# Reordering the first loads of a strided-attention kernel: keys, first Q block, values, and 8 KiB runs for two blocks

## The chip, the cores and the metric

The kernel runs on one core of a Trainium2 chip. Its engines have short names in the profile: PE multiplies matrices, DVE and POOL work on vectors, ACT applies functions such as exp, and SP issues the DMAs, the transfers between the chip's memory and the core. 16 DMA engines share each large transfer; a transfer has *landed* when all of them have reported their share. The metric is the device time of one execution in microseconds (us). Its profile has a span a little shorter than that time (128.5 us of 130.28 us in the profiled run of the kernel before). Times are medians of several executions. A ratio is the mean time of one kernel's fast runs divided by the mean time of the other's fast runs of the same rounds, so it is not quite the ratio of the medians quoted.

## The reference

```python
batch, heads, seq, dim = (8, 12, 1024, 64)          # Q, K, V: float32, stride = 64
scale = 1.0 / np.sqrt(dim)
for i in range(seq):                                # every query
    attend_positions = np.arange(0, seq, stride)    # ... sees the same 16 positions
    scores  = einsum('bhqd,bhkd->bhqk', q_i, k[attend_positions]) * scale
    weights = softmax(scores)                       # max subtracted, 1e-10 in the denominator
    result[:, :, i, :] = einsum('bhqk,bhkd->bhqd', weights, v[attend_positions])
```

Q and the result are 25.2 MB each. Of K and V only 16 rows per head are used, 0.39 MB each, but each row is a run of only 256 bytes. Per byte moved there is little arithmetic.

## The kernel before

The 96 heads are taken in 24 groups of four. Per group the kernel loads 1 MiB of Q, transposes it on PE, forms scores, takes exp on ACT, sums and multiplies by the values on PE, scales on DVE and stores 1 MiB. All DMAs are issued by SP, in program order, on one queue. Eleven Q buffers let eleven loads be issued ahead.

```python
kv_src = [[stride * D, P], [2 * HG * SD, NC], [1, D]]       # 128 x 12 runs of 256 bytes
nc.sync.dma_start(k_raw, _ap_with(K, kv_src))
nc.sync.dma_start(v_raw, _ap_with(V, kv_src))
def load(g):                                                # 1 MiB of Q in 32 runs of 32 KiB
    qn[g] = qn_pool.tile([P, 32 * D], FP32, name="qn", tag="qn")
    _copy(nc, qn[g], _ap_with(Q, [[HG * SD // 32, 32], [1, HG * SD // 32]], g * HG * SD))
for g in range(QBUFS):                                      # QBUFS = 11
    load(g)
# ... on POOL: identity, perm_k, k_dup (needs K), perm_v, v_bf (needs V), iota (leads to mask) ...
# ... PE: kp from k_dup; then vp from v_bf, four matmuls with two PSUM buffers,
#     each emptied by four DVE instructions (v_bd) that also need mask ...
for g in range(2):
    for x in range(2):
        transposes(g, x)                                    # PE, then an ACT copy to qt
scores(0)                                                   # PE, then exp on ACT
for g in range(NG):                                         # NG = 24
    sums(g)
    outputs(g, 0)
    outputs(g, 1)
    if g + 1 < NG:
        scores(g + 1)
    # ... outputs(g, 2), outputs(g, 3), transposes(g + 2, 0 and 1) ...
    store(g)                                                # 1 MiB
    if g + QBUFS < NG:
        load(g + QBUFS)
```

The softmax here doesn't subtract the row's maximum and nothing guards it: scores larger than these inputs give would overflow.

## Time and profile before

| | before |
|---|---|
| median of all its runs beside the changed kernel's first six | 130.32 us (130.23 to 130.45) |
| span of the profiled run | 128.5 us |
| busiest compute engine | ACT, 67% of the span |
| DMA engines' packet time | 96.3% of 16 engines' span |
| first store issued | 25.18 us |
| last DVE instruction ends | 114.22 us |

These are the page's slices of the kernel before (40 equal slices of 3.2 us; a digit is the busy share in tenths, GB/s is what the 16 DMA engines moved) and its queue table (packets, MB, share of 16 engines' span).

```profile
DVE  6229963787677777787777877877877778750000
ACT  2163294988889888898888898888988888400000
DMA  2999989999899899999999999999998999999980
GB/s 57 351 398 418 449 367 490 388 423 439 339 421 487 357 441 439 413 434 449 383 467 426 393 459 428 393 469 421 405 469 357 416 434 416 421 428 421 434 337 23
q1 hardware_dynamic: 7712, 51.12, 96.3%
q8 instruction: 7, 0.11, 0.4%
q14 instruction: 3, 0.02, 0.0%
```

The DMA row is full from the second slice on, and it goes on for three slices after DVE has stopped. The last two rows are instruction fetches, and the page counts them among the packets of the 16 DMA engines.

The start of the kernel and the end of its compute, from the timelines of SP, POOL, PE and DVE (start in us, duration in us, engine, line, operation, operands; in brackets the idle time before it and what ended it):

```profile
1.99 12.62 SPq L34 DMA_DIRECT2D qn<-in_Q_dram  x11
5.06 1.60 POOL L116 CAST k_dup<-k_raw 128x768 bf16<-128x768 f32 x2 [3.04 <-DMA k_raw<-in_K_dram]
7.80 0.83 POOL L124 CAST v_bf<-v_raw 128x768 bf16<-128x768 f32 x1
9.68 8.49 DVE L180 TENSOR_SCALAR v_bd<-vp,mask 128x384 bf16<-128x384 f32 x16
14.29 1.91 PE L193 MATMUL qt_ps<-identity,qn 128*128 128x128 bf16 x16
25.18 0.63 SPq L34 DMA_DIRECT2D out_dram<-out_sb  x1
111.74 2.48 DVE L243 TENSOR_TENSOR out_sb<-o_ps,rec 128x512 f32<-128x512 f32 x4
```

The last row is the end of DVE's work (111.74 + 2.48 = 114.22 us). The cast of V starts without a wait, because POOL was still busy when V landed. The first transposes start at 14.29 us although Q block 0 had landed at 9.2 us: PE issues the fourth value matmul first, and that waits for DVE.

The chain of waits of this kernel, and the longest waits of SP (waiter, what it waited for, us in total, times, longest):

```profile
ACT 60%; PE 13%; DVE 5%; DMA 3%; POOL 3%; issue 2%; ACTq 1%; DVEq 0%; POOLq 0%
SPq L34 <- DMA qn<-in_Q_dram: 25.3, 15, 2.0
SPq L34 <- DMA out_dram<-out_sb: 22.6, 13, 2.0
SPq L34 <- DVE out_sb L243: 20.0, 12, 3.3
SPq L34 <- DVE rec L231: 19.3, 7, 8.8
SPq L307 <- DMA out_dram<-out_sb: 12.6, 1, 12.6
```

The chain names ACT, but the last line decides: after everything has been computed and issued, SP waits 12.6 us for stores to land. The chain followed compute back from the last instruction and doesn't see the backlog of DMA work. Compute has slack, and the DMA engines have none.

### The profile page before, as it was taken

How to read it: one execution, taken by the hardware profiler on the slowest of the kernel's cores; microseconds unless marked ns; L12 is line 12 of the kernel's file. 1: busy time of each engine (PE TensorE's matmuls, PEld its weight loads, DVE VectorE, ACT ScalarE, POOL GpSimd, SP SyncE). 2: the span in 40 equal slices, each digit the busy share in tenths (PEclk: the TensorE clock that was granted, in tenths of full speed). 3: DMA queues.
4: the chain of work that ended last, by engine and by line, in shares of the span. 5: the costliest groups of instructions: out<-in, count | busy, mean ns of one | idle time of the engine just before them, and what ended most of it. 6: DMA issues, size and time to landing. Idle time of an engine off the chain costs nothing.

```text
span 128.5 us, 2215 instructions
## 1 busy us (share of the span) xinstructions
PE 69.4 (54%) x880; PEld 51.1 (40%) x880; DVE 83.7 (65%) x144; ACT 86.3 (67%) x103; POOL 5.1 (4%) x23
## 2 busy tenths in 40 slices
PE   0071665975656866558766578665687655510000
PEld 0040542754445654445544456443465444300000
DVE  6229963787677777787777877877877778750000
ACT  2163294988889888898888898888988888400000
POOL 4470000000000000000000000000000000000000
PEclk9999997799999999999999999999999999955555
DMA  2999989999899899999999999999998999999980
GB/s 57 351 398 418 449 367 490 388 423 439 339 421 487 357 441 439 413 434 449 383 467 426 393 459 428 393 469 421 405 469 357 416 434 416 421 428 421 434 337 23
DMA packets 7722, 51.26 MB, mean 399 GB/s; under 512 B 3872, under 2 KB 3872, under 8 KB 3872
## 3 DMA queue, kind: packets, MB, share of 16 engines
q1 hardware_dynamic: 7712, 51.12, 96.3%
q8 instruction: 7, 0.11, 0.4%
q14 instruction: 3, 0.02, 0.0%
HBM read 25.95 MB, written 25.17 MB: 398 GB/s over the span
## 4 chain that ended last, share of the span: by engine, by line
ACT 60%; PE 13%; DVE 5%; DMA 3%; POOL 3%; issue 2%; ACTq 1%; DVEq 0%; POOLq 0%
ACT qt L198 34%; ACT w L218 26%; PE sc L206 8%; DVE v_bd L180 3%; DMA k_raw<-in_K_dram 3%; PE qt_ps L193 2%; PE o_ps L238 2%; DVE out_sb L243 1%; POOL k_dup L116 1%; POOL perm_v L120 1%; PE sm L227 1%; POOL v_bf L124 1%; ACTq L307 1%; DVEq L307 0%; PE vp L175 0%
## 5 line engine op out<-in xcount | busy, mean ns | idle before, releaser
L243 DVE TENSOR_TENSOR out_sb<-o_ps,rec 128x512 f32<-128x512 f32 x96 | 63.3, 688 | 15.3 <-PE o_ps L238 12.9
L198 ACT COPY qt<-qt_ps 128x1024 bf16<-128x1024 bf16 x48 | 46.2, 1015 | 5.2 <-PE qt_ps L193 4.7
L218 ACT ACTIVATE w<-sc 64x512 bf16<-64x512 f32 x48 | 35.4, 737 | 13.2 <-PE sc L206 12.9
L238 PE MATMUL o_ps<-v_bd,w 128*128 128x256 bf16 x192 | 33.4, 278 | 0.6 <-DVE out_sb L243 0.6
L193 PE MATMUL qt_ps<-identity,qn 128*128 128x128 bf16 x384 | 30.7, 227 | 0.2 <-ACT qt L198 0.2
L193 PEld LDWEIGHTS <-qn 128*128 128x128 bf16 x384 | 27.0, 102 | 3.9 <-issue 2.6
L206 PE MATMUL sc<-qt,k_t 128*32 128x512 bf16 x96 | 9.8, 395 | 24.5 <-ACT qt L198 24.5
L238 PEld LDWEIGHTS <-w 128*128 128x128 bf16 x192 | 14.3, 98 | 6.9 <-issue 6.2
L206 PEld LDWEIGHTS <-k_t 128*32 128x32 bf16 x96 | 4.4, 93 | 29.3 <-issue 29.2
L231 DVE RECIPROCAL rec<-sm 128x32 f32<-128x32 f32 x24 | 8.6, 358 | 9.0 <-PE sm L227 9.0
L227 PE MATMUL sm<-s_sel,w 128*128 128x4 bf16 x192 | 8.5, 166 | 6.9 <-ACT w L218 6.9
L227 PEld LDWEIGHTS <-w 128*128 128x128 bf16 x192 | 6.4, 96 | 11.0 <-ACT w L218 11.0
L180 DVE TENSOR_SCALAR v_bd<-vp,mask 128x384 bf16<-128x384 f32 x16 | 8.5, 608 | 0.1
L166 ACT CAST k_t<-kp 64x512 bf16<-64x512 f32 x6 | 3.5, 579 | 3.6 <-PE kp L160 3.5
L160 PE MATMUL kp<-perm_k,k_dup 128*128 128x128 bf16 x12 | 1.5, 312 | 6.7 <-POOL k_dup L116 6.7
L175 PE MATMUL vp<-v_bf,perm_v 128*128 128x384 bf16 x4 | 1.8, 490 | 4.6 <-DVE v_bd L180 4.1
L160 PEld LDWEIGHTS <-k_dup 128*128 128x128 bf16 x12 | 1.2, 145 | 6.7 <-POOL k_dup L116 6.7
L138 DVE TENSOR_SCALAR slot_i<-iota_p 128x1 int16<-128x1 int16 x1 | 0.2, 156 | 4.7 <-POOL iota_p L136 4.7
L166 ACT ACT_TABLE_LOAD x1 | 1.3, 1283 | 2.5 <-DVE k_t L127 2.5
L127 DVE MEMSET k_t<- 128x1536 uint32 x1 | 1.3, 1338 | 1.1 <-PEq L293 1.1
L175 PEld LDWEIGHTS <-perm_v 128*128 128x128 bf16 x4 | 0.5, 127 | 3.7 <-issue 3.7
L116 POOL CAST k_dup<-k_raw 128x768 bf16<-128x768 f32 x2 | 1.6, 827 | 3.0 <-DMA k_raw<-in_K_dram 3.0
(15 smaller groups left out, 6.0 us busy)
## 6 DMA issues: line engine op xcount, KB each, us to landing
qn<-in_Q_dram SPq DMA_DIRECT2D x24, 1024.0 KB, 19.0
out_dram<-out_sb SPq DMA_DIRECT2D x24, 1024.0 KB, 19.5
k_raw<-in_K_dram SPq DMA_DIRECT2D x1, 384.0 KB, 4.3
v_raw<-in_V_dram SPq DMA_DIRECT2D x1, 384.0 KB, 5.4
```

Source lines behind the costliest of these rows:

```text
L116: nc.gpsimd.tensor_copy(out=k_dup[:, :, e], in_=k_raw)
L160: nc.tensor.matmul(kp[:, i], lhsT=k_dup[:, 4 * n + i].rearrange("p e d -> p (e d)"), rhs=pk, start=True, stop=True,)
L166: nc.scalar.copy(k_t[h, 4 * n : 4 * n + 4, :, :, e].rearrange("p n c s k -> p (n c s) k"), kp[h].rearrange("p n c s k -> p (n c s) k"),)
L180: nc.vector.tensor_scalar(out=v_bd[:, 6 * n : 6 * n + 6, c, s], in0=vp, scalar1=mask[:, s : s + 1], scalar2=None, op0=ALU.mult,)
L193: nc.tensor.transpose(ps[:, i], _ap_with(qb, [qb.ap[0], [2, P]], extra_offset=(8 * x + i) * 2 * P + 1), identity,)
L198: nc.scalar.copy(qt[g][:, x], ps)
L206: nc.tensor.matmul(sc[32 * j : 32 * j + 32], lhsT=kt[:, 32 * j : 32 * j + 32], rhs=_ap_with(q, [q.ap[0], [P, 8], [8 * P, 2], [1, 32]], ext ...
L218: nc.scalar.activation(out=_ap_with(wa, [wa.ap[0], [P, 8], [1, 2], [2, 32]], extra_offset=64 * a), in_=sc[64 * a : 64 * a + 64].rearrange( ...
L227: nc.tensor.matmul(sm[:, :, i], lhsT=wt[g][:, i], rhs=s_sel, start=True, stop=True)
L231: nc.vector.reciprocal(rec[g], sm.rearrange("p b i e -> p b (i e)"))
L238: nc.tensor.matmul(ps[:, :, i], lhsT=wt[g][:, 2 * c + i], rhs=v_bd[:, g // 2, g % 2].rearrange("p s d -> p (s d)"), start=True, stop=True,)
L243: nc.vector.tensor_tensor(out=out_sb[g][:, :, 4 * c : 4 * c + 4], in0=ps.rearrange("p b i (e d) -> p b (i e) d", e=2), in1=rec[g][:, :, 4 ...
```

## The change

The intent is that the first Q block and the keys arrive early, ahead of the values, and that the first two Q blocks are read in smaller runs, so that the first transposes could begin sooner.

```diff
-    nc.sync.dma_start(k_raw, _ap_with(K, kv_src))
-    nc.sync.dma_start(v_raw, _ap_with(V, kv_src))
     def load(g):
         qn[g] = qn_pool.tile([P, 32 * D], FP32, name="qn", tag="qn")
-        _copy(
-            nc, qn[g], _ap_with(Q, [[HG * SD // 32, 32], [1, HG * SD // 32]], g * HG * SD)
-        )
-    for g in range(QBUFS):
+        n = P if g < 2 else 32
+        _copy(nc, qn[g], _ap_with(Q, [[HG * SD // n, n], [1, HG * SD // n]], g * HG * SD))
+
+    nc.sync.dma_start(k_raw, _ap_with(K, kv_src))
+    load(0)
+    nc.sync.dma_start(v_raw, _ap_with(V, kv_src))
+    for g in range(1, QBUFS):
         load(g)
```

The order of instructions on PE, DVE, ACT and POOL is unchanged; only SP's issues move.

## The prediction

> **What bounds the kernel now.** The DMA engines. The page's slices show DMA at 9 tenths nearly everywhere from 2 to 126 us; the queue table puts 51.12 MB on one queue whose packets fill 96.3% of 16 engines' span; the windows view shows 414 to 434 GB/s between 26 and 80 us. Compute isn't the limit, although the chain of waits is 60% ACT: ACT does one group in 3.94 us, while a group's load and store take about 2 x 2.45 us of DMA. The last eviction ends at 114.2 us, then SP waits 12.6 us for stores (waits of SP): that is compute's slack.
>
> DMA is weak only at the start: nothing moves until about 1.84 us, and K and V, in 256-byte runs (3072 packets), run at 197 GB/s in 2-4 us. Such a packet took about 18 ns (up to 27 among Q packets), so K and V hold each engine 3.9 us for 0.79 MB. The Trainium skill ("DMA: Bandwidth & Descriptors", Why small descriptors are slow) gives such a per-packet cost; the trace agrees in direction.
>
> **What the change does.** Instruction order on PE, DVE, ACT and POOL is unchanged; only SP's issues move. Bytes and 256-byte packets are unchanged.
> - 64 packets of 32 KiB (1219 ns each) become 256 of 8 KiB (stores' take 311 ns): 1244 against 1219 ns, 25 ns x 4 per engine, +0.1 us, if 8 KiB loads cost what stores do.
> - K lands about 5.0 us as before. Q block 0 lands about 7.3 us instead of 9.2. V lands about 9.0 instead of 6.6: 1 MiB (2.5 us) is now ahead of it.
> - Earlier Q buys nothing: PE runs four value matmuls before the transposes, and the fourth waits for DVE v_bd. Transposes start at 14.3 us, Q long landed.
> - Later V costs. The v_bf cast started at 7.80 us because POOL was busy; now it waits for V. iota and mask follow on POOL. So v_bd starts about 10.9 instead of 9.68, transposes about 15.5, the first store about 26.4 instead of 25.18: compute 1.2 us later throughout.
>
> **How much is on the critical path.** Nearly none. At 25.2 us the queue still holds about 7 us of Q loads (11 x 2.45 us after K and V, to about 33 us), so a first store 1.2 us late leaves no gap. At the end the backlog shrinks from 12.6 to about 11.4 us. At most 8 DMAs are in flight (issues wait for landings), as before. What can change is DMA work: V's small packets no longer run among 32 KiB packets, so some of the 62.9 us of 256-byte packet time (3.9 us an engine, 3.4 at 18 ns) may go: 0 to 0.5 us, against +0.1.
>
> **Predicted: 130.1 us, range 129.3 to 130.9.** Faster by over 2%: 0.03; within 2%: 0.95; slower by over 2%: 0.02.
>
> **What would show the steps right or wrong.** Right: v_raw lands 2 us or more later; POOL waits about 1 us for it; v_bd, transposes and first store start about 1.2 us later, and every later compute step too; SP's final wait shrinks by about 1.2 us; the last store lands within 0.5 us of before. Wrong: DMA below 8 tenths in some slice between 20 and 40 us, or the final wait unchanged while compute shifts.
>
> **What would make it wrong.** 8 KiB reads going at another rate than 8 KiB stores; V's small packets, behind Q block 0, packing differently by over a microsecond; a microsecond's shift of stores against loads changing the mixed rate (slices vary from 339 to 490 GB/s).

## The result, and the profile after

The changed kernel took 130.63 us (median of six, 130.25 to 130.74) against 130.32 us (130.23 to 130.45). The ratio is 1.0016, 95% interval 1.0000 to 1.0032: the same within 2%, with a hint of slower. Six further runs in the experiments gave 130.62 us and a ratio of 1.0025 (1.0013 to 1.0037), so the hint came back, about 0.2% (over those six runs 0.31 us of time, 0.30 us of it inside the span). It is at the edge of what these runs resolve: on another chip a kernel with this same order of DMAs (after_early, below) gave 0.9999, and kernels with the old order gave anything from 0.9985 to 1.0021.

The same views as before, of the changed kernel:

```profile
DVE  6207990987787777877777877778778778660000
ACT  2173078788898888898888988888988889400000
DMA  2999989989799899899999999999999999999960
GB/s 69 372 324 455 488 346 468 437 371 488 335 422 503 335 442 480 356 450 442 381 473 401 399 447 422 412 432 442 404 440 404 427 422 427 419 424 427 424 277 13
q1 hardware_dynamic: 7904, 51.12, 95.8%
```

```profile
4.85 1.60 POOL L116 CAST k_dup<-k_raw 128x768 bf16<-128x768 f32 x2 [2.83 <-DMA k_raw<-in_K_dram]
9.14 0.83 POOL L124 CAST v_bf<-v_raw 128x768 bf16<-128x768 f32 x1 [1.50 <-DMA v_raw<-in_V_dram]
11.02 8.49 DVE L180 TENSOR_SCALAR v_bd<-vp,mask 128x384 bf16<-128x384 f32 x16
15.64 1.91 PE L193 MATMUL qt_ps<-identity,qn 128*128 128x128 bf16 x16
25.75 0.63 SPq L34 DMA_DIRECT2D out_dram<-out_sb  x1
112.45 2.48 DVE L243 TENSOR_TENSOR out_sb<-o_ps,rec 128x512 f32<-128x512 f32 x4
```

```profile
SPq L34 <- DVE out_sb L243: 30.1, 12, 9.2
SPq L34 <- DMA qn<-in_Q_dram: 22.0, 13, 2.0
SPq L34 <- DMA out_dram<-out_sb: 19.6, 11, 2.1
SPq L34 <- DVE rec L231: 16.4, 9, 3.3
SPq L307 <- DMA out_dram<-out_sb: 12.4, 1, 12.4
```

POOL now waits 1.50 us for V, and v_bd and the transposes start 1.34 and 1.35 us later. Q block 0 came about 1.8 us earlier (7.4 us), and nothing used it. SP waits longer for DVE (46.5 us in the two rows against 39.3) and less for landings: compute is later, and the DMA queue is a little less full. The last DVE instruction ends at 114.93 us, 0.71 us later.

**Which DMA engine ends last.** The trace records, for every DMA, the moment at which each of the 16 DMA engines reported its share as landed. For the last store these 16 moments are the ends of the 16 engines' work. Worked out from those records (us from the start of the span; one profiled run per kernel):

```
kernel          mean of 16  second last    last    last - mean   V's landing relative to Q block 0
before              125.38       126.56  127.50           2.12   ahead
runs_only           125.37       126.06  127.55           2.18   ahead
late_1              125.37       126.51  127.57           2.20   ahead
late_2              125.43       126.79  127.63           2.20   ahead
before_early        125.53       126.79  127.65           2.12   ahead
after               125.27       125.95  127.96           2.69   behind
after_again         125.38       126.16  127.77           2.40   behind
order_only          125.35       126.31  128.03           2.68   behind
after_early         125.22       125.78  127.91           2.68   behind
no_sums             125.03       125.86  126.84           1.81   behind
q_first             125.97       126.59  128.44           2.47   (Q block 0 ahead of K and V)
v_after_3           126.61       127.58  128.83           2.22   (V behind three Q blocks)
```

The average engine of the changed kernel ended 0.11 us earlier than in the kernel before, roughly as predicted. One single engine ended 0.46 us later, and that one ends the kernel. In the second profile of the changed kernel (after_again) the mean was the same as before and the last engine 0.27 us later. The profiled runs of after and order_only were the slowest of their six, so these rows lean to the slow side. In every run here one engine lands 1.8 us or more behind the mean. (pool_1000 and last_store_15 are told below.)

### The profile page after: what moved, and what is told of

It reads as the page before. It is cut to its first block, busy times and chain, and to the rows that moved or that the text cites. A ratio compares the mean times of both kernels' runs of the same rounds, so it can differ in the third digit from the quotient of the medians.

```text
span 129.0 us, 2215 instructions
## 1 busy us (share of the span) xinstructions
PE 70.5 (55%) x880; PEld 51.9 (40%) x880; DVE 83.6 (65%) x144; ACT 86.3 (67%) x103; POOL 5.1 (4%) x23
## 4 chain that ended last, share of the span: by engine, by line
ACT 59%; PE 13%; DVE 6%; issue 4%; DMA 3%; POOL 2%; POOLq 1%; ACTq 1%; DVEq 1%
ACT qt L198 33%; ACT w L218 26%; PE sc L206 7%; DVE v_bd L180 3%; DMA k_raw<-in_K_dram 3%; PE qt_ps L193 3%; PE o_ps L238 2%; DVE out_sb L243 1%; POOL k_dup L116 1%; POOL perm_v L120 1%; PE sm L227 1%; POOLq L307 1%; ACTq L307 1%; DVEq L307 0%; PE vp L175 0%
## 5 line engine op out<-in xcount | busy, mean ns | idle before, releaser
L218 ACT ACTIVATE w<-sc 64x512 bf16<-64x512 f32 x48 | 35.3, 736 | 12.6 <-PE sc L206 12.3
L193 PE MATMUL qt_ps<-identity,qn 128*128 128x128 bf16 x384 | 31.6, 231 | 0.2 <-ACT qt L198 0.2
L193 PEld LDWEIGHTS <-qn 128*128 128x128 bf16 x384 | 27.6, 104 | 3.7 <-issue 2.6
```

Of the source, the lines that this page charges most:

```text
L193: nc.tensor.transpose(ps[:, i], _ap_with(qb, [qb.ap[0], [2, P]], extra_offset=(8 * x + i) * 2 * P + 1), identity,)
L218: nc.scalar.activation(out=_ap_with(wa, [wa.ap[0], [P, 8], [1, 2], [2, 32]], extra_offset=64 * a), in_=sc[64 * a : 64 * a + 64].rearrange( ...
```

## The experiments

Theory A: compute's delay is absorbed by the backlog of DMA work, so the time is set by the DMA engines alone, and the residue of 0.3 us by which engine carries the instruction fetches. Theory B: the delay of compute costs by itself. Theory C: 8 KiB loads cost more than 32 KiB loads. All kernels below had three or more fast runs, timed beside the kernel before on the same chip.

### after_again: the changed kernel unchanged

> The changed kernel again, unchanged, for the spread of its runs. Its first six runs fell in two clusters (130.25 and 130.28; 130.61 to 130.74), those of before in one (130.23 to 130.45). Theory A (the DMA engines' work is the same; which engine happens to carry the instruction fetches decides the last landing by some tenths of a us): again a spread of about 0.5 us, mean 0.1 to 0.3 us above before. Theory B (the later V and first store cost something by themselves): the profiled run shows DMA engines idle somewhere between 10 and 120 us. Theory C (8 KiB loads cost more than 32 KiB loads): the same, without idle time, but with longer packets.

Measured: 130.62 us (130.51 to 131.01), ratio 1.0025 (1.0013 to 1.0037). The first store was issued at 26.84 us in this profile, 1.1 us later than in the first one, and the time was the same. The two clusters of the first six runs did not come back.

### order_only and runs_only: the two halves of the change

```diff
 order_only:  -        n = P if g < 2 else 32
              +        n = 32
 runs_only:   -    load(0)
              -    nc.sync.dma_start(v_raw, _ap_with(V, kv_src))
              -    for g in range(1, QBUFS):
              +    nc.sync.dma_start(v_raw, _ap_with(V, kv_src))
              +    for g in range(QBUFS):
```

> Order K, Q block 0, V as in the change, but every Q block in 32 KiB runs. A: the same as before within 0.3 us. B: as slow as the changed kernel (ratio about 1.0016 or more), with v_bd starting about 11.0 us as there. C: as fast as before or faster by 0.1 to 0.2 us (V's packets cost less away from the others), ratio 0.999 to 1.000.

> Order K, V, Q as before, the first two Q blocks in 8 KiB runs. v_bd should start about 9.7 us and the first store about 25.2 us as before. A: the same as before within 0.3 us. B: exactly before, ratio 1.000. C: ratio about 1.0016.

Measured: order_only 130.65 us (130.30 to 130.94), ratio 1.0021 (1.0007 to 1.0034); runs_only 130.43 us (130.41 to 130.68), ratio 1.0010 (0.9998 to 1.0022). The order alone gives a ratio as high as the whole change did. The run length makes nothing that these runs can show, and C falls as the main cause; the two intervals overlap, so a small share of it isn't ruled out. In packet times, too, run length is nearly free: the 8 KiB and 32 KiB packets together took 1910.5 us of engine time before and 1911.1 us after, which is 0.03 us for each of 16 engines (0.04 in runs_only, 0.15 in after_again).

### q_first: Q block 0 ahead of K as well

```diff
+    load(0)
     nc.sync.dma_start(k_raw, _ap_with(K, kv_src))
-    load(0)
     nc.sync.dma_start(v_raw, _ap_with(V, kv_src))
```

> Q block 0 ahead of both K and V. K lands about 2.5 us later (about 7.3 us), so all compute should start about 2.5 us later than in before and the first store come near 28 us; that is still before the first loads run out at about 33 us. A: the same within 0.4 us of before, perhaps 0.3 us faster, because the slow first microsecond of the DMA (a ramp with engines half idle from 1.9 to 2.9 us) might be shorter with 8 KiB packets than with 256-byte ones. B: slower than the changed kernel by about as much again (ratio about 1.003 or more).

Measured: 131.22 us (131.08 to 131.30), ratio 1.0064 (1.0052 to 1.0076). B's number came true, but the trace shows another reason for most of it. Here the 256-byte packets of K and V follow one another with Q packets ahead and behind, and took 4.24 us of each engine instead of 3.93 (before) and 3.60 (after). The mean landing was 0.57 us later already at the fourth transfer, when the same bytes had come in (11.95 against 11.38 us), and it is 0.59 us later at the end, two thirds of the 0.89 us between the medians. The hoped-for shorter ramp at the start did not appear (106 GB/s from 1.9 to 2.9 us against 96 before). Because this run changed the DMA work and the delay together, it could not separate A from B; late_1 and late_2 were made for that.

### late_1 and late_2: a delay of compute with the DMA order of before

```diff
+    scratch = const.tile([P, 1], FP32, name="scratch")
+    for _ in range(13):                       # 26 in late_2
+        nc.gpsimd.memset(scratch, 0.0)
     v_bf = const.tile([P, NC, D], BF16, name="v_bf")
     nc.gpsimd.tensor_copy(out=v_bf, in_=v_raw)
```

> The kernel before, its DMA order untouched, with 13 tiny memsets (about 0.1 us each) on POOL ahead of the value cast, so that all compute starts about 1.3 us later, as in the changed kernel. Theory A (a delay of compute is absorbed; the order of the DMAs or chance moves the last landing): ratio to before 1.000, at most 1.001. Theory B (a delay of compute moves the end by itself): ratio 1.002, as the changed kernel.

> The same with 26 memsets, compute about 2.6 us late, as in the kernel with Q block 0 ahead of K. A: ratio 1.000 to 1.001, so that the 0.9 us of that kernel come from its DMA order (its mean last landing was 0.6 us later). B: more than the first, ratio 1.003 to 1.006.

The POOL and DVE timelines and the final wait of SP in late_1:

```profile
7.76 1.99 POOL L125 MEMSET scratch<- 128x1 f32 x13
9.69 0.83 POOL L127 CAST v_bf<-v_raw 128x768 bf16<-128x768 f32 x1
11.56 8.49 DVE L183 TENSOR_SCALAR v_bd<-vp,mask 128x384 bf16<-128x384 f32 x16
27.02 0.63 SPq L34 DMA_DIRECT2D out_dram<-out_sb  x1
SPq L310 <- DMA out_dram<-out_sb: 10.8, 1, 10.8
```

Measured: late_1 130.28 us (130.25 to 130.43), ratio 0.9985 (0.9973 to 0.9998). The thirteen memsets took 1.99 us, so compute was 1.9 us late, more than in the changed kernel, and the first store was 1.84 us later. SP's final wait fell from 12.6 to 10.8 us, by the same 1.8 us, and the time did not rise. This is the clean test, and B falls for a delay of this size. (That it came out 0.15% *faster* can't be the delay's doing; it shows how little a difference of that size in one batch means.)

late_2: 130.69 us (130.63 to 130.99), ratio 1.0021 (1.0009 to 1.0034), with v_bd at 13.71 us, 4.0 us late. Its mean of last landings (125.43) and its last landing (127.63) are within 0.13 us of the kernel before, and its span is 128.6 us against 128.5 us. Over all its runs the time is 0.30 us longer than in the kernel before and the span 0.08 us, so most of the extra lies outside the span. The trace has one more instruction fetch at 130.5 us, after the span's end, which no other kernel here has; whether that is the cause was not tested.

### v_after_3: V behind three Q blocks

```diff
-    load(0)
+    for g in range(3):
+        load(g)
     nc.sync.dma_start(v_raw, _ap_with(V, kv_src))
-    for g in range(1, QBUFS):
+    for g in range(3, QBUFS):
         load(g)
```

> As the changed kernel, but V is loaded after Q blocks 0, 1 and 2. V should land near 14 us, so all compute starts about 5 us later than in the changed kernel (6.3 us later than before); the first store near 31.5 us, still ahead of the end of the first loads (about 33.5 us), and the last store issued near 120 us with the DMA engines still behind it. Theory A (compute's delay is absorbed; the DMA engines' work and the one engine that lands last set the time): ratio to before 1.000 to 1.004. Theory B (a delay of compute costs by itself: 1.3 us of it cost 0.3 us): the cost grows with the delay, to about 1.4 us, ratio about 1.011.

The windows view of v_after_3 and then of the kernel before (stretch in us, its length, busy time of PE, PEld, DVE, ACT, POOL, granted clock, DMA share, GB/s):

```profile
32.00:34.00 2.00, 1.54 (x22) 1.28 (x22) 1.90 (x4) 1.49 (x3) 0.00 (x0) 1.00 0.74 303
34.00:36.00 2.00, 1.17 (x19) 0.78 (x17) 1.64 (x4) 1.98 (x3) 0.00 (x0) 1.00 1.27 397
36.00:38.00 2.00, 1.54 (x22) 1.27 (x22) 1.43 (x4) 1.42 (x3) 0.00 (x0) 1.00 1.19 373
38.00:40.00 2.00, 1.11 (x18) 0.72 (x16) 1.57 (x4) 1.98 (x3) 0.00 (x0) 1.00 0.60 234
```

```profile
32.00:34.00 2.00, 0.81 (x12) 0.60 (x13) 1.56 (x4) 1.98 (x3) 0.00 (x0) 1.00 0.69 283
34.00:36.00 2.00, 1.84 (x24) 1.39 (x23) 1.43 (x3) 1.49 (x3) 0.00 (x0) 1.00 1.40 594
36.00:38.00 2.00, 0.81 (x12) 0.60 (x13) 1.64 (x4) 1.98 (x3) 0.00 (x0) 1.00 0.70 299
38.00:40.00 2.00, 1.84 (x24) 1.39 (x23) 1.43 (x3) 1.49 (x3) 0.00 (x0) 1.00 0.95 397
```

Measured: 131.46 us (130.64 to 132.39), ratio 1.0080 (1.0039 to 1.0121), a wide spread. This goes against A's number, and the trace shows where A's slack ended. Single windows bunch large packets (283, then 594), so read the mean of the four: 327 GB/s here against 393 before. The first store was issued at 31.47 us, and the eleven first loads ended at about 33.8 us (mean of the engines). In the next 5 us the packets themselves were slow: the 32 KiB loads took a median of 1666 ns instead of 1218, and the slowest tenth of the stores' 8 KiB packets 646 to 695 ns instead of 311. The mean of the last landings is 1.23 us later. The reading is that a delay is absorbed only while the DMA queue is well filled when the first stores come, and that a lead of 2 us was not enough. It is argued, because this run too changed the DMA order and the delay together. In late_2 the lead was about 5.6 us (first store at 28.29 us), and its large packets took no longer in all than those of the kernel before (1910.3 against 1910.5 us); in the changed kernel it was about 7 to 8 us.

### after_early and before_early: compute earlier

```diff
 # both: iota_p and col4 are computed ahead of v_bf on POOL; vp takes the PSUM buffers of the outputs
-    # four value matmuls and their v_bd
-    for g in range(2):
-        for x in range(2):
-            transposes(g, x)
-    scores(0)
+    transposes(0, 0); transposes(0, 1)                        # after_early
+    values(0, 0); values(0, 1); values(1, 0)                  # (before_early: these first)
+    transposes(1, 0); transposes(1, 1); scores(0)
+    values(1, 1)
```

> The changed kernel's DMA order, with compute started earlier: index constants ahead of the value cast on POOL, the transposes of Q block 0 ahead of the value matmuls on PE (here the early Q block 0 is used), those of block 1 between them. The first store should be issued near 24 us instead of 25.8 to 26.8. A: as the changed kernel, ratio to before 1.000 to 1.003. B: the cost of the change goes away, ratio 0.997 to 1.000.

> The DMA order of before with compute started earlier by the same means (value matmuls first, since V lands first here). The first store should be issued near 22 us instead of 25.2. A: ratio to before 0.999 to 1.001. B: faster than before, ratio 0.993 to 0.998; it would be the fastest kernel of all.

Measured: after_early 130.42 us (130.02 to 130.78), ratio 0.9999 (0.9981 to 1.0016), first store at 22.06 us. before_early 130.26 us (130.16 to 130.43), ratio 0.9986 (0.9974 to 0.9998), first store at 21.43 us. Compute started up to 3.7 us earlier than in its parent kernel, with no gain that stands out from the spread: before_early equals late_1, which is 1.8 us late instead of 3.7 us early. From 3.7 us early to 1.9 us late, the time doesn't depend on when compute starts by more than these batches scatter. after_early's mean would fit B's story for the changed kernel, but its runs are spread over 0.76 us and its profiled run (130.76 us, its second slowest) has the same late last engine as the other kernels of that order, so it settles nothing about the 0.2%.

### pool_1000 and no_sums: more and fewer instructions

```diff
 pool_1000:  +    for _ in range(1000):
             +        nc.gpsimd.memset(scratch, 0.0)
 no_sums:    -        for i in range(8):
             -            nc.tensor.matmul(sm[:, :, i], lhsT=wt[g][:, i], rhs=s_sel, start=True, stop=True)
             +        nc.tensor.matmul(sm.rearrange("p b i e -> p (b i e)"), lhsT=wt[g][:, 0],
             +                         rhs=ones, start=True, stop=True)
```

> The changed kernel with 1000 tiny memsets of a scratch tile added on POOL, which is idle after 11 us: no wait depends on them. They add instructions, and so instruction fetches, but no bytes of data. Theory A (instruction fetches on the DMA engines decide which engine lands last): more instruction packets on the DMA table, and the time above the changed kernel's by 0.3 to 1.5 us (ratio to before 1.004 to 1.014). If fetches don't matter: as the changed kernel, ratio 1.002.

> The changed kernel with one matmul a group in place of the eight that sum the weights (a wrong result on purpose: the quotient is not the sum of the right block). It takes 336 of 1762 instructions from PE, so about one or two of seven instruction fetches. Theory A: the same or slightly faster than the changed kernel, ratio to before 0.996 to 1.002. Compute as the limit would give more, since about 0.4 us a group of PE work goes.

pool_1000 failed as a measure of time: 168.81 us (ratio 1.2947), because POOL itself became the longest chain (its 1000 memsets end at about 166 us). Its DMA records can still be read. Queue 14 had eleven instruction packets instead of three:

```profile
q8 instruction: 7, 0.11, 0.3%
q14 instruction: 11, 0.09, 0.1%
```

Its 16 last landings were: fourteen at 125.96 us or earlier, one at 127.93 and one at 129.01 us. In the changed kernel the last two were 125.95 and 127.96 us. Rank by rank, fourteen engines ended about as before and the last two 2.0 and 1.1 us later. Of the eight added fetches six came before the last landing, so this fits fetches that fall on few engines; it is one profile, and which engines they were isn't recorded.

no_sums took 130.03 us (129.62 to 130.18), ratio 0.9964 (0.9950 to 0.9978), 0.5 to 0.6% under the changed kernel that it was made from when each is compared with the kernel before on its own chip (ratios 1.0016 and 1.0025), 0.7 to 0.8 us. Its output is wrong, which doesn't matter for the time. Its queue 8 had five fetches instead of seven:

```profile
q8 instruction: 5, 0.08, 0.2%
```

The mean of its last landings fell by 0.24 us and the last one by 1.12 us. It also takes work from PE, but its compute was not earlier for that: the first store came at 26.47 us and DVE's last instruction ended at 115.60 us, against 25.75 and 114.93. And late_1 and before_early show that such shifts don't matter here. So the fetches remain as the reason; this last step is argued.

How much one fetch costs an engine can be estimated by pairing each engine's successive landings in the kernel before, which normally lie 2.46 us apart. After the 16 KiB fetches of queue 8, one engine's interval was longer by about 1.1 to 1.7 us, a different engine each of the seven times; after the 8 KiB fetches of queue 14 by 0.6 to 0.8 us (the pairing is a reconstruction; the records don't name the engines). The same pairing says which engine ends last: the one that two fetches fell on. In the kernel before it was set back by 1.57 us after the fetch at 83.1 us and by 0.73 us after the one of queue 14 at 99.8 us; in the changed kernel by 1.74 us (fetch at 28.1 us) and 0.75 us (100.6 us). One sign of it needs no pairing: in each of the twelve kernels of the table, just after queue 14's last fetch inside the span (at 99 to 106 us), one transfer's last landing came 2.78 to 3.45 us after that of the transfer before, where its neighbours have 2.3 to 2.7.

The Trainium skill says in "Runtime: NRT & Kernel Launch", Instruction fetch mechanics, that each engine's instructions are refilled in 16 KiB blocks of 256, by a DMA queue of its own. For PE the trace is near that: its 1760 instructions (6.9 blocks) come with seven fetches of 16,384 bytes on queue 8, and 1424 (5.6 blocks) with five. For POOL it differs: the fetches that 1000 memsets added were eight of 8,192 bytes, 125 memsets to a fetch, and they came on queue 14, which carries three fetches in the kernel before too, from 44.8 us on, long after POOL has stopped. The page calls the cost "mostly hidden". In this kernel, which DMA limits, it is not hidden, by the estimates above.

### last_store_15: taking the last rows off one engine

```diff
-        _copy(nc, <rows 0 to 127 of out>, <rows 0 to 127 of out_sb>)
+        for r, n in [(0, P)] if g < NG - 1 else [(0, 120), (120, 8)]:
+            _copy(nc, <rows r to r+n of out>, <rows r to r+n of out_sb>)
```

> The kernel before, with its last store split in rows 0 to 119 and rows 120 to 127, so that the DMA engine that holds the last eight rows of a 128-row transfer should carry eight packets (2.5 us) less at the end, and eight others one more each (0.3 us). If the engine that lands last (about 2.1 us behind the mean of the 16 last landings) is that one, the time falls by 1.0 to 1.6 us (ratio 0.988 to 0.992). If it is another, the time stays or grows by up to 0.3 us plus the cost of one more DMA (ratio 1.000 to 1.004).

Measured: 131.11 us (130.65 to 131.44), ratio 1.0054 (1.0038 to 1.0070), on the base of the kernel before. The guess was wrong. The last of the 15 shares of the large part landed at 128.15 us, and the last extra row 0.32 us later, at 128.47 us, about the time of one packet. By this the late engine is among the eight that were given an extra row, and it got more work instead of less. Why the large part's last share came 0.65 us later than the whole store's in the kernel before isn't known. I found no safe way to give it less with transfers of this form.

No version beat both kernels by more than the spread. The lowest times of a correct kernel, 130.26 and 130.28 us, lie within 0.2 us of those of the kernel before (130.32 to 130.45).

## Why the prediction was right

- *DMA is the limit, compute has slack.* Right (though the windows view also has 400 GB/s, from 30 to 40 us, below the 414 to 434 of the prediction). late_1 delayed compute by 1.9 us; SP's final wait took the 1.8 us and the time stayed.
- *V lands about 9.0 us; v_bd 10.9, transposes 15.5.* Right: the cast of V waited until 9.14, v_bd started at 11.02, transposes at 15.64.
- *First store about 26.4 us, compute 1.2 us later throughout.* The size was off, both ways: 25.75 us and 0.71 us at the end in one profile, 26.84 us and 1.8 us in the other. The start moved by 1.3 us in the first; what came after varied. In the windows view the granted clock was 0.50 from 22 to 24 us before and from 24 to 26 us after, so it fell on other work; that this is the reason is argued.
- *The final wait shrinks to about 11.4 us.* It measured 12.4. The sum is 12.6 - 0.71 (compute later) + 0.46 (last landing later) = 12.35. In the second profile compute was 1.8 us later, and the wait was 11.1.
- *256-byte packets save 0 to 0.5 us.* Right: their engine time fell from 62.9 to 57.6 us, 0.33 us an engine. But these packets overlap, so packet time isn't elapsed time: once K, V and Q block 0 were in, the mean landing was at 8.90 us before and at 8.78 and 8.88 us in the two profiles after, a gain of 0.12 and 0.01 us (0.11 and 0.00 at the end). *8 KiB runs cost 0.1 us.* They cost 0.03 and 0.15.
- *So 130.1 us.* The range held 130.63, but the small net step had the wrong sign. The step that failed is "What can change is DMA work", taken as a sum over the engines divided by 16. The mean engine ended 0.11 us earlier in the first profile and at the same time in the second. The kernel ends with its last engine, which ended 0.46 us later in the first profile and 0.27 us later in the second. The instruction fetches had been in the queue table from the start, at 0.4%, and I had not asked which engines they fall on.
- *DMA below 8 tenths between 20 and 40 us would show a step wrong.* The sign appeared (a 7 in the slice from 32.3 to 35.5 us), but it was a bad sign. Over 32 to 36 us the windows view gives 438 GB/s before and 436 after; large packets bunch in short slices.

What stays open is why the order K, Q block 0, V should give a later last engine, if it does. In one profile of each kernel the gap between the last engine and the mean is 2.12 to 2.20 us in all five kernels with V ahead of Q block 0, and 2.40 to 2.69 us in the four with V just behind it and the full program. But v_after_3, with V further behind, has 2.22 us, and two of the four profiles are the slowest runs of their kernels, so the pattern is weak. Among the nine the gap follows neither the run length (order_only, runs_only) nor the time at which compute starts (late_1, after_early). The link from load order to gap was not found, and at 0.2% it is near what these runs can resolve.

## What to carry to other kernels

Where one queue of loads and stores is full from beginning to end, the order of the first loads and the start of compute changed little here (0.2% in this change, 0.6% with Q block 0 ahead of K), as long as the first stores came well before the first loads ran out; the wait for stores at the very end is the measure of that slack. The end of such a kernel is the end of its slowest DMA engine and not of the average one, so look at the last landings of all engines, and count instruction fetches as DMA work that falls on one engine at a time. When a load is moved forward, check that something can use it: here the early Q block waited 8 us behind four matmuls that needed the load it had displaced.

## What the Trainium skill lacked or had wrong

- "Runtime: NRT & Kernel Launch", Instruction fetch mechanics, calls the cost of an instruction block mostly hidden. In a kernel limited by DMA each 16 KiB fetch set one DMA engine back by an estimated 1.1 to 1.7 us, and a kernel with five such fetches instead of seven ended 0.7 to 0.8 us earlier (ratios to the kernel before 0.9964 against 1.0016 and 1.0025), though it also did less on PE. The page has blocks of 16 KiB for each engine; POOL's came in fetches of 8,192 bytes, eight for 1000 memsets, on a queue (14) that also carried three fetches while POOL was idle.
- "DMA: Bandwidth & Descriptors" gives no figure for how unevenly the 16 engines end; its section Latency and other measured facts says only that engines 7 and 15 are usually slower than the others in traces. Here the last engine was 1.8 to 2.7 us behind the mean in the twelve kernels of the table, and 3.5 us in pool_1000 with its added fetches (the one with a split store can't be put on that scale). The records don't name the engines, so whether it was one of those two isn't known.
- "DMA: Bandwidth & Descriptors", Why small descriptors are slow, gives 27% overhead for 256-byte descriptors (3 cycles of 11). Here, from 3.3 to 3.8 us of the kernel before, 564 such packets began on 16 engines, one per 14.2 ns on each, where 256 bytes at the pace of 8 KiB packets (one every 307 ns) would take 9.6 ns: by this estimate overhead is 32% of the time. (Each took a median of 18 ns; they overlap.)
- "DMA: Bandwidth & Descriptors", Rules for kernel authors, says of few large against many small descriptors for the same bytes that the faster "has not been measured on hardware". Reading 1 MiB in 128 runs of 8 KiB instead of 32 runs of 32 KiB, for two blocks of 24, gave a ratio of 1.0010 (0.9998 to 1.0022) and 0.04 us of packet time an engine: no difference that shows.
